# A list scheduler's latencies, landing time, buffer names and order table exchanged in a four-layer attention step

## The chip, the cores and the metric

The kernel runs on one core of a Trainium2 chip. The metric is device time in microseconds (us) of one execution; the median of three runs counts. The engines are named as the profile names them: PE is TensorE's matmuls, PEld its weight loads, DVE is VectorE, ACT is ScalarE, POOL is GpSimd, and SP issues every transfer of this kernel from one queue.

## The reference

One step of a model with four layers over 128 context tokens and 512 latent tokens of width 1024, all in float32. Layers 0 and 3 attend globally, layer 1 in a band with a sink logit, layer 2 in a two-dimensional neighbourhood with a bias table. Cut to what matters:

```python
for l in range(DEPTH):                      # the context tokens, then the latent ones
    shift, scl, gate = split(silu(cond) @ w_mod[l] + b_mod[l])
    u = rms_norm(h, norm_pre[l]) * (1 + scl) + shift
    q, k, v, z = split(u @ w_in[l])         # q: 16 heads of 64, k and v: 4 heads of 64
    q, k = rms_norm(q), rms_norm(k)         # per head; rotary positions for latent tokens
    o = softmax(q k^T / 8 [+ mask or bias]) v     # latent queries also read cached k and v
    h = h + gate * rms_norm((o * silu(z)) @ w_out[l], norm_post[l])
    # ... (k and v of the context tokens go out as a new cache)
```

## The kernel before

The 640 tokens are five tiles (tau) of 128; tile 0 is the context. The parts of a layer are functions named in `S.named`: `kv` projects k and v and stacks the transposed keys into `kst` (`k_stack`, its transposes are L553), `qt` projects and transposes q (products L497, transposes L620) for one half c of the heads, `z` makes the gate (L634), `pv` holds scores (L698, L724), softmax (maximum L701, exponential L703, scaling L658), the transposes of the probabilities p (L773) and the product with v (L780), `cx` does the context's heads (L800, L826, L834), `og` splits gated results, `no` and `out` multiply by w_out (L901), `un` and `up` normalize and shift the next layer's input (`mad` in `start_part`, L461 on ACT, L463 on DVE). `mod` and `mf` are the products with w_mod (L383; L346 for the first half of layer 0's), which need `cpad`, made from the tiny input `cnd` (L280, L282, L284, L285).

Float32 products are done as three products of a high and a low part. Each weight chunk of 128x512 comes into a `raw` tile, ACT rounds it (L261), DVE or POOL subtracts (L262). A PSUM result is copied out by ACT or DVE (`evac`, L256). There are four PSUM tiles `B`, two double ones `S`, and six `raw` tiles.

The program is not written in the order in which it runs. Every `S.op` lists the engines that could do a piece of work, with a price. `Sched.emit` then plays a list scheduler with these prices: it takes for each engine the ready operation with the least (start, key), where the key is the operation's number plus `ORDER[part]`, `MODSHIFT` or `SSHIFT`; it looks at most `WINDOW` operations ahead; a result counts as ready after the latency `LAT` of the pair of engines, a transfer so long after its end on the queue's model; `SLACK` favours keys over early starts, and `DISLIKE` handicaps a form of work on an engine that has an alternative (Ap and mada on ACT; V, V2 and mad on DVE; G and G1 on POOL). What it picks is emitted at once, so the playing decides each engine's order, SP's too, and which engine does what. At run time each engine keeps that order and waits by semaphores. Buffers of a kind come from a pool; the kernel's model only counted how many were free.

Of the kernel before, what the change touches and what calls it, by code (L numbers as in the profile page):

```python
# [25 lines left out]
           (([(0, (0, 2))], [(1, (0, 2))], [(0, (2, 4))], [(1, (2, 4))]),))  # L26


ORDER = {'hn': -470, 'up': -310, 'pv': 20, 'nat': 90, 'tab': -80, 'un': -170, 'bt': -280, 'st': -780, 'out': 230,
         'z': 90, 'og': -200, 'sc': 180, 'qt': -410, 'no': 180, 'ks': -170, 'mod': 160, 'w': -60}  # L30
MODSHIFT = 100
SSHIFT = -200
WINDOW = 520
PLAT = 270
XLAT = 180
SLACK = {'P': 140, 'V': 0, 'A': 220, 'G': 50, 'D': 80}
DISLIKE = {'Ap': 1060, 'mada': 3020, 'G1': 980, 'mad': 900, 'V': 1260, 'V2': 960, 'G': 780}
CAPS = {'p': 6, 'raw': 6, 'cap_prep': 3}
NEG = -1e30
KINDS = [0, 1, 2, 0]  # L40
# [7 lines left out]
class Buf:  # L48


    def __init__(self, tag, shape, dt):
        self.tag, self.shape, self.dt = tag, shape, dt
        self.ap = None
        self.ops = 0
        self.freed = 0.0
        self.hist = []


class Sched:

    LAT = {("P", "P"): 0, ("V", "V"): 130, ("A", "A"): 155, ("G", "G"): 110, ("P", "V"): 200, ("P", "A"): 200,
           ("G", "V"): 80, ("A", "V"): 110, ("V", "A"): 135, ("G", "A"): 150, ("D", "D"): 100, ("V", "P"): 235, ("A", "P"): 228}

# [58 lines left out]
    def emit(self):  # L126
# [5 lines left out]
            for d in deps:  # L132
                users[d].append(i)
        free = {e: 0.0 for e in "PVAGD"}
        slots = {t: [0.0] * c for t, (c, _) in self.tags.items()}
        done, where = [None] * n, [None] * n
        port = 0.0
        pend = {e: [] for e in "PVAGD"}
# [8 lines left out]
        out, low, last = 0, 0, "M"  # L147
        while out < n:
            while where[low]:
                low += 1  # L150
            best = None
            for e, lst in pend.items():
                cand = None
                for x in lst:
                    i = x[1]
                    if i > low + WINDOW or self.prev[i] is not None and where[self.prev[i]] is None:
                        continue
                    if x[3] is None:
                        t = 0.0
                        for d in self.ops[i][1]:  # L160
                            t = max(t, done[d] + (self.LAT.get((where[d], e), PLAT if e == "P" else XLAT)))
                        x[3] = t
                    t = max(x[3], free[e] + (self.TURN.get((last, x[2][3]), 0) if e == "P" else 0))
                    if e == "G" or x[2][3] in self.SHARED:
                        t = max(t, port)
                    need = {}
                    for b in self.ops[i][2]:
                        if b.ap is None:
                            m = need[b.tag] = need.get(b.tag, 0) + 1
                            s = slots[b.tag]  # L170
                            t = max(t, s[m - 1]) if len(s) >= m else 1e18
                    if t < 1e17:
                        key = (max(t, free[e] + SLACK[e]), x[0])
                        if cand is None or key < cand[0]:
                            late = DISLIKE.get(x[2][3], 0) if len(self.ops[i][0]) > 1 else 0
                            cand = (key, t, x, t + late)
                if cand and (best is None or cand[3] < best[0][3]):
                    best = (cand, e)
            if best is None:
                raise RuntimeError("no op can go")  # L180
            (_, t, x, _), e = best
            i, (_, dur, fn, _) = x[1], x[2]
            for alt in self.ops[i][0]:
                pend[alt[0]] = [y for y in pend[alt[0]] if y[1] != i]
            for b in self.ops[i][2]:
                if b.ap is None:
                    slots[b.tag].pop(0)
                    b.ap = self.tags[b.tag][1](b)
            fn(self.eng[e])
            free[e] = t + dur  # L190
            if e == "G" or x[2][3] in self.SHARED:
                port = t + dur
            if e == "P":
                last = x[2][3]
            done[i] = t + dur + (2000 if e == "D" else 0)
            where[i] = e
            for b in self.ops[i][2]:
                b.ops -= 1
                b.freed = max(b.freed, done[i])
                if not b.ops:  # L200
                    bisect.insort(slots[b.tag], b.freed + (215 if b.tag in ("S", "B") else 150))
            out += 1
            for u in users[i]:
                left[u] -= 1
                if not left[u]:
                    ready(u)


def build(ctx, tc, a, o):
# [5 lines left out]
    S = Sched(nc)  # L215

    def sbuf_tag(name, cap):
        S.tag(name, cap, lambda b: sb.tile(b.shape, b.dt, tag=name, name=name, bufs=cap))

    def psum_tag(name, cap):  # L220
        S.tag(name, cap, lambda b: pp.tile(b.shape, b.dt, tag=name, name=name, bufs=cap))

    for name, cap in (("gate", 1), ("q", 5), ("kst", 1), ("kn2", 1), ("vt", 1), ("w", 8),
                      ("raw", 4), ("p", 5), ("pt", 6), ("tmp", 6), ("tab", 1), ("gt", 1), ("modc", 4), ("bcol", 4),
# [738 lines left out]
    mod = mod_tile(0)  # L963
# [111 lines left out]
```

## Time and profile before

| what | value |
|---|---|
| runs | 1398.53, 1402.02, 1402.59 us; median 1402.02 |
| the profiled execution | 1400.58 us, of which 1398.5 us are the span from first to last instruction |
| PE busy | 1357.7 us, 97% of the span |
| PEld busy | 1122.3 us, 80% |
| DVE, ACT, POOL busy | 954.7, 758.6, 266.8 us (68, 54, 19%) |
| transfers | 145.11 MB, mean 104 GB/s |

A line of groups (such as "PE MATMUL B<-w,uB ... x816") has the engine, the operation, what it writes and reads, and how often. A timeline row has the start in us, the length in us, the engine, the kernel's line, and in brackets how long the engine sat idle before it and whose end released it. A matmul's end is modelled, so that a wait shorter than a matmul's pipeline does not show as idle time.

### The profile page before, as it was taken

The page shows a single profiled execution, that of the slowest core. Times are in us where ns is not written, and L with a number is a line of the kernel's source. Part 1 is how long each engine was busy: PE and PEld are TensorE (multiplying, and loading weights), DVE is VectorE, ACT ScalarE, POOL GpSimd, SP SyncE. Part 2 cuts the span into 40 slices and gives each one's busy share as a digit, 9 for nine tenths or more (in the row PEclk, how much of TensorE's full clock was granted, in tenths as well). Part 3 has the DMA queues.
Part 4 walks back from the last instruction along what each step waited for, and adds up shares of the span by engine and source line. Part 5 has one row for each costly group of instructions (what it writes and reads, how often), then busy time and mean ns, then how long its engine had stood idle before and what let it go on. Part 6 is the DMA issues. An engine that isn't in the chain of part 4 may idle for free.

```text
span 1398.5 us, 25496 instructions
## 1 busy us (share of the span) xinstructions
PE 1357.7 (97%) x9464; PEld 1122.3 (80%) x9464; DVE 954.7 (68%) x2300; ACT 758.6 (54%) x1854; POOL 266.8 (19%) x306
## 2 busy tenths in 40 slices
PE   6999999999999999999999999999999999999998
PEld 3788887888778887887878888888778888778876
DVE  4777667765587786777486676578488876577653
ACT  4556565554355565666354567468345555465641
POOL 1122012010032102201033541441033210021100
PEclk9999999999999999999999999999999999999999
DMA  8522222224532402324542522342633210111032
GB/s 305 175 69 84 61 91 84 69 87 140 181 115 67 147 30 91 125 92 161 161 125 73 157 57 91 98 141 85 196 126 101 91 53 10 61 52 41 31 123 103
DMA packets 73323, 145.11 MB, mean 104 GB/s; under 512 B 8752, under 2 KB 13936, under 8 KB 73200
## 3 DMA queue, kind: packets, MB, share of 16 engines
q1 hardware_dynamic: 73200, 143.50, 31.6%
q8 instruction: 74, 1.21, 0.4%
q14 instruction: 49, 0.40, 0.1%
HBM read 131.90 MB, written 11.57 MB: 103 GB/s over the span
## 4 chain that ended last, share of the span: by engine, by line
PE 83%; DVE 6%; ACT 4%; DMA 3%; issue 3%; POOL 0%; SPq 0%; DVEq 0%; POOLq 0%; ACTq 0%
PE B L497 21%; PE B L634 14%; PE B L780 8%; PE B L773 8%; PE S L901 8%; PE B L901 6%; PE S L698 5%; PE S L724 4%; PE B L383 3%; PE B L620 2%; PE S L497 1%; DVE w L262 1%; DMA raw<-in_w_mod 1%; DMA raw<-in_w_in 1%; PE B L451 1%
## 5 line engine op out<-in xcount | busy, mean ns | idle before, releaser
L307 POOL TENSOR_TENSOR sm<-sm,mhalf 128x1 f32<-128x1 f32 (+2 forms) x100 | 122.1, 1223 | 573.2 <-DVE sm L302 291.5
L497 PE MATMUL B<-w,uB 128*128 128x512 f32 x816 | 207.4, 401 | 0.0
L256 ACT ACTIVATE pt<-B 128x512 f32<-128x512 f32 (+1 forms) x228 | 126.9, 570 | 121.0 <-PE B L773 110.8
L497 PEld LDWEIGHTS B<-w,uB 128*128 128x128 f32 x816 | 149.2, 188 | 31.8 <-DVE uB L262 0.4
L634 PE MATMUL B<-uB,w 128*128 128x384 f32 x768 | 166.0, 348 | 0.6 <-DVE gate L642 0.3
L773 PE MATMUL B<-ident,p 128*128 128x128 f32 x1088 | 159.4, 276 | 3.1 <-ACT pt L256 2.3
L261 ACT ACTIVATE w<-raw 128x512 fp32r<-128x512 f32 x224 | 135.0, 627 | 30.2 <-PE B L901 8.0
L773 PEld LDWEIGHTS B<-ident,p 128*128 128x128 f32 x1088 | 125.1, 141 | 23.7 <-issue 13.6
L262 DVE TENSOR_TENSOR w<-raw,w 128x512 fp32r<-128x512 f32 x193 | 130.5, 700 | 13.0 <-ACT w L261 12.4
L497 PE MATMUL B<-w,uA 128*128 128x512 f32 x528 | 135.1, 403 | 1.1 <-DVE pt L256 0.8
L703 ACT ACTIVATE p<-S,sm 128x640 f32<-128x640 f32 x128 | 101.3, 794 | 59.6 <-DVE sm L701 54.6
L780 PE MATMUL B<-pt,vt 128*64 128x256 f32 (+1 forms) x1152 | 133.0, 376 | 0.0
L634 PEld LDWEIGHTS B<-uB,w 128*128 128x128 f32 x768 | 129.6, 188 | 3.7 <-issue 1.5
L701 DVE TENSOR_REDUCE sm<-S 128x1 f32<-128x640 f32 x128 | 102.7, 819 | 37.7 <-PE S L698 36.8
L634 PE MATMUL B<-uA,w 128*128 128x256 f32 x768 | 117.6, 290 | 0.3 <-DVE modc L394 0.3
L497 PEld LDWEIGHTS B<-w,uA 128*128 128x128 f32 x528 | 96.4, 188 | 24.7 <-DVE w L262 2.1
L780 PEld LDWEIGHTS B<-pt,vt 128*64 128x64 f32 x1152 | 77.5, 137 | 46.0 <-issue 11.4
L634 PEld LDWEIGHTS B<-uA,w 128*128 128x128 f32 x768 | 102.5, 189 | 3.4 <-issue 1.8
L658 DVE TENSOR_SCALAR p<-p,sm 128x640 f32<-128x640 f32 (+2 forms) x197 | 96.9, 506 | 6.6 <-DVE sm L657 0.5
L698 PE MATMUL S<-kst,q 128*128 128x320 f32 x512 | 96.8, 320 | 2.9 <-ACT p L703 2.8
L658 POOL TENSOR_SCALAR p<-p,sm 128x640 f32<-128x640 f32 (+2 forms) x59 | 44.0, 751 | 284.3 <-DVE sm L657 236.4
L737 ACT ACTIVATE p<-p,sm 128x512 f32<-128x512 f32 (+1 forms) x128 | 83.9, 657 | 6.4 <-DVE sm L735 6.3
(148 smaller groups left out, 2216.1 us busy)
## 6 DMA issues: line engine op xcount, KB each, us to landing
raw<-in_w_in SPq DMA_DIRECT2D x160, 256.0 KB
raw<-in_w_mod SPq DMA_DIRECT2D x160, 256.0 KB
raw<-in_w_out SPq DMA_DIRECT2D x64, 256.0 KB
w<-in_w_first SPq DMA_DIRECT2D x16, 512.0 KB
xs<-q SPq DMA_DIRECT2D x15, 512.0 KB
q<-xs SPq DMA_DIRECT2D x15, 512.0 KB
q<-in_x SPq DMA_DIRECT2D x10, 512.0 KB
kst<-gs SPq DMA_DIRECT2D x8, 512.0 KB
```

The source lines that it names most:

```text
L256: alts = {"A": Ap(n, lambda e: e.activation(out(), in_(), AF.Copy)), "V": V(n, lambda e: e.tensor_copy(out(), in_()))}
L261: S.op([As(n, lambda e: e.activation(h(), src(), AF.Copy))], r, w)
L262: f = lambda e: e.tensor_sub(l(), src(), h().bitcast(F32))
L307: S.op([("G", 395 + 157 * n, lambda e: e.tensor_tensor(r.ap, v.ap, mhalf.ap.to_broadcast([128, n]), op=OP.pow), "pow")], r=[v, mhalf], w=[r])
L497: e.matmul(ps(), t.ap[:, s, k, off:off + 128], W[k].ap[:, w], start=k == 0 and i == 0, stop=k == 7 and i == 2)
L634: e.matmul(ps.ap[:, 0:w], W[k].ap[:, wi, 128 * f:128 * f + 128], t.ap[:, s, k, :], start=k == 0 and i == 0, stop=k == 7 and i == 2)
L658: f = lambda e, i=i, p=p, w=w: e.tensor_scalar(p.ap[:, 0:w], p.ap[:, 0:w], rs.ap[:, i:i + 1], 1.0, op0=OP.mult, op1=OP.mult)
L698: e.matmul(ps.ap[:, b, 0:320], Q[t + 1].ap[:, hh], kst.ap[:, g, s, 320 * b:320 * b + 320], start=s == 0, stop=s == 1)
L701: S.op([V(640, lambda e, ps=ps, i=i: e.tensor_reduce(negm.ap[:, i:i + 1], ps.ap[:, :, 0:320], axis=AX.XY, op=OP.max, negate=True))], r=[ps ...
L773: e.transpose(pt.ap[:, c:c + 128], p.ap[:, b:b + 128], ident.ap)
L780: e.matmul(po.ap[64 * x:64 * x + 64, 256 * half + q0:256 * half + q0 + w], vt.ap[:, kt, 64 * g:64 * g + 64], sbt.ap[:, c0:c0 + w], start=f ...
L901: e.matmul(ps(), t.ap[:, s, k, off:off + 128], W[k].ap[:, w], start=k == 0 and i == 0, stop=k == 7 and i == 2)
```

## The change

Two constants' tables that the scheduler plays with (`LAT` and what stands in the first lines) get other numbers. A transfer counts as landed 4000 ns after its issue's end in the model, not 2000. A freed buffer now carries a slot number, and each slot has a name of its own in the memory pool, so that the buffer which the model hands out is the one that the program uses. No instruction's form is new, and no work is added or removed. The diff, with two lines of the order table:

```diff
-ORDER = {'hn': -470, 'up': -310, 'pv': 20, ... 'st': -780, 'out': 230,
+ORDER = {'mf': -5, 'tab': 1033, 'kv': -1015, ... 'hn': -2276, ... 'qt':
...
-MODSHIFT = 100
-SSHIFT = -200
-WINDOW = 520
+MODSHIFT = 38
+SSHIFT = -255
+WINDOW = 750
+LAND = 4000
-SLACK = {'P': 140, 'V': 0, 'A': 220, 'G': 50, 'D': 80}
-DISLIKE = {'Ap': 1060, 'mada': 3020, 'G1': 980, 'mad': 900, 'V': 1260, 'V2': 960, 'G': 780}
+SLACK = {'P': 98, 'V': 112, 'A': 190, 'G': 158, 'D': 16}
+DISLIKE = {'V2': 437, 'V': 4793, 'Ap': 663, 'G': 1355, 'mad': 1665, 'mada': 380, 'G1': 549}
...
-    LAT = {... ("P", "V"): 200, ("P", "A"): 200, ... ("V", "P"): 235, ("A", "P"): 228}
+    LAT = {... ("P", "V"): 210, ("P", "A"): 235, ... ("V", "P"): 150, ("A", "P"): 175, ...}
...
-        slots = {t: [0.0] * c for t, (c, _) in self.tags.items()}
+        slots = {t: [(0.0, k) for k in range(c)] for t, (c, _) in self.tags.items()}
...
-                    slots[b.tag].pop(0)
+                    b.slot = slots[b.tag].pop(0)[1]
...
-            done[i] = t + dur + (2000 if e == "D" else 0)
+            done[i] = t + dur + (LAND if e == "D" else 0)
...
-                    bisect.insort(slots[b.tag], b.freed + (215 if b.tag in ("S", "B") else 150))
+                    bisect.insort(slots[b.tag], (b.freed + (170 if b.tag in ("S", "B") else 190), b.slot))
...
-        S.tag(name, cap, lambda b: sb.tile(b.shape, b.dt, tag=name, name=name, bufs=cap))
+        S.tag(name, cap, lambda b: sb.tile(b.shape, b.dt, tag="%s%d" % (name, b.slot), name=name, bufs=1))
```

Nearly every row of the order moves. In the changed program each line number is four higher. These are the places that the prediction speaks of.

**The first transfers on SP.** Before:

```order
L280 DMA cnd<-in_cond 128x16
L329 DMA bcol<-in_vec 128x40
L296 DMA sink<-in_sink 128x16
L340 DMA w<-in_w_first 128x1024 x2
L969 DMA q<-in_x 128x1024
L340 DMA w<-in_w_first 128x1024 x2
```

And changed:

```order
L569 DMA tmp<-in_cache_k 128x128
L570 DMA kn_79<-in_cache_k 128x128
L571 DMA vt<-in_cache_v 128x256
L344 DMA w<-in_w_first 128x1024 x4
L284 DMA cnd<-in_cond 128x16
L333 DMA bcol<-in_vec 128x40
L300 DMA sink<-in_sink 128x16
L973 DMA q<-in_x 128x1024
```

The tiny `cnd`, first before, now stands behind three tiles of the cache and four of 512 KB.

**PE in layer 3, where the first half of the heads ends and the key stack of the second half is transposed** (L553 before, L557 now). Before:

```order
L800 MATMUL S<-kst,q 128x128 x8
L773 MATMUL B<-ident,p 128x128 x4
L634 MATMUL B<-uA,w 128x256 x9
L800 MATMUL S<-kst,q 128x128 x8
L773 MATMUL B<-ident,p 128x128 x8
L553 MATMUL B<-identr,tmp 128x128 x8
L780 MATMUL B<-pt,vt 64x256 x10
L553 MATMUL B<-identr,tmp 128x128 x16
L634 MATMUL B<-uB,w 128x384 x9
```

And changed:

```order
L804 MATMUL S<-kst,q 128x128 x8
L501 MATMUL B<-w,uA 128x512 x3
L784 MATMUL B<-pt,vt 64x256 x10
L557 MATMUL B<-identr,tmp 128x128 x4
L501 MATMUL B<-w,uA 128x512 x3
L557 MATMUL B<-identr,tmp 128x128 x8
L501 MATMUL B<-w,uA 128x512 x3
L557 MATMUL B<-identr,tmp 128x128 x8
L501 MATMUL B<-w,uA 128x512 x3
L557 MATMUL B<-identr,tmp 128x128 x4
```

The 24 transposes, in rows of 8 and 16, now come as 4, 8, 8 and 4 with three products of the next projection between them; the p transposes that stood straight ahead of them have gone further up.

**ACT at the same place.** Before:

```order
L640 ACTIVATE gate<-B 128x256
L809 ACTIVATE p,sm<-S,sm 128x128
L544 ACTIVATE tmp<-kn_11958 128x256 x6
L256 ACTIVATE pt<-B 128x512
L809 ACTIVATE p,sm<-S,sm 128x128
L256 ACTIVATE pt<-B 128x512
L256 ACTIVATE kst<-B 128x4x128
```

And changed:

```order
L644 ACTIVATE gate<-B 128x384
L265 ACTIVATE w<-raw 128x512
L260 ACTIVATE pt<-B 128x512
L813 ACTIVATE p,sm<-S,sm 128x128
L548 ACTIVATE tmp<-kn_11397 128x256 x6
L813 ACTIVATE p,sm<-S,sm 128x128 x3
L265 ACTIVATE w<-raw 128x512
L813 ACTIVATE p,sm<-S,sm 128x128
L260 ACTIVATE kst<-B 128x4x128
```

Two copies of transposed probabilities (`pt`) stood behind the six conversions of keys; now the last of them stands ahead.

**PE in layer 3, where the second half's scores begin.** Before:

```order
L698 MATMUL S<-kst,q 128x320 x4
L634 MATMUL B<-uA,w 128x256 x12
L773 MATMUL B<-ident,p 128x128 x4
L620 MATMUL B<-identr,tmp 128x128 x4
L634 MATMUL B<-uA,w 128x256 x6
L620 MATMUL B<-identr,tmp 128x128 x4
L698 MATMUL S<-kst,q 128x320 x4
L634 MATMUL B<-uB,w 128x384 x6
L383 MATMUL B<-raw,cpad 32x128 x16
```

And changed:

```order
L702 MATMUL S<-kst,q 128x320 x4
L638 MATMUL B<-uA,w 128x256 x9
L638 MATMUL B<-uB,w 128x384 x9
L638 MATMUL B<-uA,w 128x256 x3
L638 MATMUL B<-uB,w 128x384 x3
L638 MATMUL B<-uA,w 128x256 x6
L638 MATMUL B<-uB,w 128x384 x3
L638 MATMUL B<-uA,w 128x256 x6
L638 MATMUL B<-uB,w 128x384 x9
L624 MATMUL B<-identr,tmp 128x128 x8
L702 MATMUL S<-kst,q 128x320 x8
L777 MATMUL B<-ident,p 128x128 x4
L387 MATMUL B<-raw,cpad 32x128 x16
```

Between one score group and the next stood 18 gate products and two sets of transposes; now 48 gate products stand there, and the w_mod product (L383, now L387) comes later among them.

Which engine does a piece also changes. Of the 160 `mad` pieces of 128x128 all ran on DVE; 144 now run on ACT. ACT does 94 more copies out of PSUM, which is all that DVE did. DVE takes 24 subtractions (L262), 21 scalings (L658) and 8 small pieces from POOL. The matmuls are the same 8104 in both programs.

## Rows read from the trace of the kernel before

**Rows 1.** The page's span, its first part (busy us, share of the span, instructions) and the chain that ended last by engine.

```profile
span 1398.5 us, 25496 instructions
PE 1357.7 (97%) x9464; PEld 1122.3 (80%) x9464; DVE 954.7 (68%) x2300; ACT 758.6 (54%) x1854; POOL 266.8 (19%) x306
PE 83%; DVE 6%; ACT 4%; DMA 3%; issue 3%; POOL 0%; SPq 0%; DVEq 0%; POOLq 0%; ACTq 0%
```

**Rows 2.** Busy time of each engine in stretches that make up the span: the stretch, its length, then each engine's busy us, the granted clock, the transfers' share and GB/s.

```profile
0.00:50.00 50.00, 37.94 (x240) 24.15 (x240) 28.82 (x87) 21.20 (x53) 7.08 (x14) 1.00 0.85 302
50.00:200.00 150.00, 147.78 (x1131) 124.71 (x1130) 110.80 (x243) 88.99 (x208) 25.89 (x23) 1.00 0.24 77
200.00:250.00 50.00, 47.58 (x323) 39.46 (x322) 30.07 (x62) 24.47 (x51) 11.70 (x8) 1.00 0.26 84
250.00:1100.00 850.00, 841.50 (x5843) 697.65 (x5842) 595.78 (x1535) 473.48 (x1193) 188.27 (x227) 1.00 0.35 111
1100.00:1250.00 150.00, 141.51 (x1051) 118.42 (x1053) 102.44 (x207) 83.66 (x189) 23.09 (x19) 0.99 0.19 60
1250.00:1391.80 141.80, 141.40 (x890) 117.91 (x890) 84.58 (x166) 66.09 (x159) 10.18 (x14) 1.00 0.21 71
1391.80:1398.50 6.70, 0.01 (x1) 0.00 (x0) 2.23 (x4) 0.69 (x2) 0.55 (x1) 0.76 0.21 78
```

**Rows 3.** What PE waited for over the whole span: who waited, for whom, us in total, times, longest us.

```profile
PE B L346 <- DMA w<-in_w_first: 6.6, 2, 6.5
PE B L383 <- DMA raw<-in_w_mod: 3.4, 6, 1.2
PE S L698 <- ACT p L703: 2.8, 4, 1.0
PE B L773 <- ACT pt L256: 2.3, 5, 0.7
PE B L553 <- ACT pt L256: 1.9, 2, 1.6
```

**Rows 4.** The start: a stretch as in rows 2, then single rows of the timelines of ACT, DVE and PE.

```profile
6.00:12.00 6.00, 4.72 (x36) 1.76 (x36) 0.92 (x4) 1.60 (x5) 0.56 (x1) 1.00 1.03 387
2.35 0.22 ACT L282 ACTIVATE th<-cnd 128x16 f32<-128x16 f32 x1 [0.35 <-DMA cnd<-in_cond]
...
4.77 0.17 DVE L285 TENSOR_TENSOR cpad<-th,cnd 128x16 f32<-128x16 f32 x1
...
6.45 1.08 PE L346 MATMUL B<-w,cpad 128*32 128x256 f32 x8 [6.45 <-DMA w<-in_w_first]
7.71 1.08 PE L346 MATMUL B<-w,cpad 128*32 128x256 f32 x8 [0.17 <-DMA w<-in_w_first]
...
13.78 1.02 PE L353 MATMUL B<-sel,pm 128*128 128x2 f32 x4 [1.23 <-ACT pm L256]
...
17.01 1.65 PE L497 MATMUL S<-w,uA 128*128 128x512 f32 x3 [1.69 <-ACT uA L261]
...
22.41 0.66 PE L451 MATMUL B<-ident,q 128*128 128x128 f32 x2 [1.39 <-issue]
...
26.56 0.94 PE L497 MATMUL S<-w,uA 128*128 128x512 f32 x3
```

**Rows 5.** The end of the first half of the heads in layer 3: PE's timeline, then ACT's, then a stretch as in rows 2.

```profile
1191.76 0.53 PE L553 MATMUL B<-identr,tmp 128*128 128x128 f32 x4 [1.56 <-ACT pt L256]
...
1193.05 3.76 PE L780 MATMUL B<-pt,vt 128*64 128x256 f32 x20
...
1198.15 1.02 PE L553 MATMUL B<-identr,tmp 128*128 128x128 f32 x8 [0.36 <-ACT kst L256]
...
1205.54 3.08 PE L497 MATMUL B<-w,uA 128*128 128x512 f32 x12 [0.78 <-DVE pt L256]
...
1189.26 1.96 ACT L544 ACTIVATE tmp<-kn 128x256 fp32r<-128x256 f32 x6
1191.10 0.61 ACT L256 ACTIVATE pt<-B 128x512 f32<-128x512 f32 x1
...
1190.00:1200.00 10.00, 7.58 (x49) 4.93 (x48) 3.82 (x11) 7.09 (x22) 0.00 (x0) 0.83 0.00 0
```

**Rows 6.** PE's timeline where the second half's scores begin in layer 3, and one row of the first half's end with the same 20 products of p and v.

```profile
1242.73 0.54 PE L620 MATMUL B<-identr,tmp 128*128 128x128 f32 x4 [0.69 <-ACT pt L256]
...
1245.46 0.86 PE L698 MATMUL S<-kst,q 128*128 128x320 f32 x4 [0.96 <-ACT p L703]
...
1249.18 0.43 PE L383 MATMUL B<-raw,cpad 128*32 128x128 f32 x8 [1.24 <-DMA raw<-in_w_mod]
...
1182.38 2.38 PE L780 MATMUL B<-pt,vt 128*64 128x256 f32 x20
```

**Rows 7.** Groups of DVE, ACT and POOL by line and shape: busy us, mean ns of one, and the idle time before them.

```profile
L463 DVE TENSOR_SCALAR tmp<-B,modc 128x128 f32<-128x128 f32 x160 | 54.6, 401 | 8.1 <-PE B L451 7.9
L256 DVE COPY pt<-B 128x512 f32<-128x512 f32 x71 | 48.2, 685 | 12.9 <-PE B L773 11.4 <-PE B L826 0.7
L262 DVE TENSOR_TENSOR w<-raw,w 128x512 fp32r<-128x512 f32 x193 | 130.5, 700 | 13.0 <-ACT w L261 12.4
L256 ACT ACTIVATE pt<-B 128x512 f32<-128x512 f32 x169 | 100.2, 598 | 111.4 <-PE B L773 101.5 <-PE B L826 8.5
L256 ACT ACTIVATE pm<-B 128x128 f32<-128x128 f32 x11 | 3.0, 277 | 16.8 <-PE B L383 16.8
```

More of the change, by code (lines that the diff above doesn't have):

```diff
@@ L26 @@
            (([(0, (0, 2))], [(1, (0, 2))], [(0, (2, 4))], [(1, (2, 4))]),))
-ORDER = {'hn': -470, 'up': -310, 'pv': 20, 'nat': 90, 'tab': -80, 'un': -170, 'bt': -280, 'st': -780, 'out': 230,
-         'z': 90, 'og': -200, 'sc': 180, 'qt': -410, 'no': 180, 'ks': -170, 'mod': 160, 'w': -60}
-MODSHIFT = 100
-SSHIFT = -200
-WINDOW = 520
+ORDER = {'mf': -5, 'tab': 1033, 'kv': -1015, 'ks': -282, 'nat': 95, 'hn': -2276, 'mod': 295, 'w': 49, 'qt':
+         -2263, 'z': 101, 'sc': 286, 'st': -268, 'pv': -2148, 'cx': 109, 'og': 2620, 'out': -950, 'no': 290,
+         'un': -513, 'up': -1539, 'bt': -809, '': 32}
+MODSHIFT = 38
+SSHIFT = -255
+WINDOW = 750
 PLAT = 270
+LAND = 4000
 XLAT = 180
-SLACK = {'P': 140, 'V': 0, 'A': 220, 'G': 50, 'D': 80}
-DISLIKE = {'Ap': 1060, 'mada': 3020, 'G1': 980, 'mad': 900, 'V': 1260, 'V2': 960, 'G': 780}
+SLACK = {'P': 98, 'V': 112, 'A': 190, 'G': 158, 'D': 16}
+DISLIKE = {'V2': 437, 'V': 4793, 'Ap': 663, 'G': 1355, 'mad': 1665, 'mada': 380, 'G1': 549}
 CAPS = {'p': 6, 'raw': 6, 'cap_prep': 3}
@@ L53, in __init__ @@
         self.ap = None
+        self.slot = 0
         self.ops = 0
@@ L59 @@
 class Sched:
-    LAT = {("P", "P"): 0, ("V", "V"): 130, ("A", "A"): 155, ("G", "G"): 110, ("P", "V"): 200, ("P", "A"): 200,
-           ("G", "V"): 80, ("A", "V"): 110, ("V", "A"): 135, ("G", "A"): 150, ("D", "D"): 100, ("V", "P"): 235, ("A", "P"): 228}
+    LAT = {("P", "P"): 0, ("V", "V"): 120, ("A", "A"): 155, ("G", "G"): 110, ("P", "V"): 210, ("P", "A"): 235,
+           ("G", "V"): 35, ("A", "V"): 145, ("V", "A"): 130, ("G", "A"): 150, ("D", "D"): 100, ("V", "P"): 150, ("A", "P"): 175,
+           ("V", "G"): 150, ("A", "G"): 190}
     TURN = {("C", "M"): 179, ("E", "M"): 179, ("C", "T"): 132, ("E", "T"): 132, ("C", "R"): 132, ("E", "R"): 132, ("R", "M"): 45,
@@ L170, in emit @@
                             s = slots[b.tag]
-                            t = max(t, s[m - 1]) if len(s) >= m else 1e18
+                            t = max(t, s[m - 1][0]) if len(s) >= m else 1e18
                     if t < 1e17:
@@ L217, in sbuf_tag @@
     def sbuf_tag(name, cap):
-        S.tag(name, cap, lambda b: sb.tile(b.shape, b.dt, tag=name, name=name, bufs=cap))
+        S.tag(name, cap, lambda b: sb.tile(b.shape, b.dt, tag="%s%d" % (name, b.slot), name=name, bufs=1))
     def psum_tag(name, cap):
-        S.tag(name, cap, lambda b: pp.tile(b.shape, b.dt, tag=name, name=name, bufs=cap))
+        S.tag(name, cap, lambda b: pp.tile(b.shape, b.dt, tag="%s%d" % (name, b.slot), name=name, bufs=1))
     for name, cap in (("gate", 1), ("q", 5), ("kst", 1), ("kn2", 1), ("vt", 1), ("w", 8),
```

## The prediction

> **What bounds the kernel now.** I read the page's first part and its chain first: PE is busy for 1357.7 of 1398.5 us, and 83% of the chain that ended last is PE's own work [rows 1]. No other engine is over 68%. The matmuls are the same 8104 in both programs, so a new order cannot shorten this work; it can only take from the 40.8 us in which PE is idle (1398.5 less 1357.7), from waits too short to show as idle, and from the slow clock that follows idleness.
>
> The second view says where these 40.8 us are [rows 2]. Per stretch, length less PE's busy time: 12.1 us in the first 50 us; 2.2 from 50 to 200; 2.4 from 200 to 250; 8.5 in all of 250 to 1100; 8.5 in the 150 us from 1100 to 1250; 0.4 up to 1391.8; and 6.7 after the last matmul. The last 6.7 us are a chain of small steps and a transfer behind the last product, the last 72 products stand in the same order in both programs, and nothing changes there. So there are 22.0 us in the middle (2.2 + 2.4 + 8.5 + 8.5 + 0.4) and 12.1 at the start that an order can touch.
>
> The third view names what ended the idle times [rows 3]: at the start the transfers of w_first (6.6 us, of which 6.5 are the first wait); in the middle many short ones, the w_mod transfers (3.4 us), the exponentials of which a score tile must be free (2.8), copies of transposed probabilities out of PSUM (2.3 and 1.9). None is a rate that something lacks: the transfers run at 0.19 to 0.35 of their capacity in the middle [rows 2]. They are places where one queue held the wrong thing first, which an order can mend.
>
> **The change, part by part.**
>
> *The start.* `cpad`, which every `mod` product needs, hangs on `cnd`. Before, `cnd` is the first transfer and ACT takes it at 2.35 us; `cpad` is made at 4.77, and PE starts at 6.45, when the first w_first tile is there; the second is used at 7.71, 1.26 us later [rows 4]. Now `cnd` stands behind four such tiles and 0.26 MB of cache. Counted from the landing at 6.45 three more tiles take 3 x 1.26 = 3.8 us, the cache 0.26 MB / 387 GB/s = 0.7 us [rows 4], so `cnd` is there at about 10.9 us. A rounding (0.22), two DVE steps (0.17 each) and three hand-overs, some 0.9 us in all, follow: PE's first w_mod product starts at about 11.8 us, 5.3 us later than before. That is one end. What comes back: by 11.8 us two products' tiles are there together and x is close behind, so the waits that PE has after its start before (0.17, 1.23, 1.69 and 1.39 us, 4.5 in all [rows 4]) have no cause left except the one of 1.23, a copy on ACT. Their sum without it is 3.3 us. PE also works in one piece sooner: until 24.9 us three products take 1.65 us and from 26.56 on 0.94 [rows 4], which is the step from the 1.2 to the 2.4 GHz level; a denser run may bring it earlier or, starting later, not. I take +5.3 - 3.3 - 0.5 = +1.5 us, with ends of +5.3 (nothing comes back) and -2 (the clock rises some us earlier, too). A small PE transposition of cached keys now goes first and costs nothing, since PE idles there.
>
> The two w_first rows at 6.45 and 7.71 are in the order of issue, but show no small transfer behind a large one [rows 4]. The Trainium skill, "DMA: Bandwidth & Descriptors", section "Two DMAs through the same engine are not ordered", says that descriptors of one queue on one engine start in order, though they may finish otherwise. By that, the tiny transfer gets the full delay of the bytes ahead, as priced above, and the trace's two rows agree; if small transfers passed large ones, the start would stay as it was, and the sum below would be 1.5 us lower.
>
> *The end of a half in layer 3.* At 1189.26 ACT takes six key conversions in a row, 1.96 us; the copy `pt` that frees a PSUM tile waits behind them until 1191.10, and PE for the copy: 1.56 us of idle, then 0.36 and 0.78 [rows 5]. And the idleness costs twice: the mean granted clock falls to 0.83 of full over 1190 to 1200 [rows 5], and the 20 products at 1193.05 take 3.76 us where the same 20 took 2.38 just before [rows 5, 6], 1.4 us lost. In the changed order the `pt` copies stand ahead of the conversions on ACT, and PE has products of the next projection between its 4, 8, 8 and 4 transposes. I take all of it away: -(1.56 + 0.36 + 0.78 + 1.4) = -4.1 us. What is late next is the copies of `kst`, 0.6 us each, against 0.7 us of products in between: no wait over some tenths.
>
> *The scores of the second half.* At 1242.73, 1245.46 and 1249.18 PE waits 0.69, 0.96 and 1.24 us [rows 6]: a copy, an exponential, a w_mod tile. The same place in layer 0 gives most of the 2.4 us of 200 to 250 [rows 2]. Now 48 gate products stand between score groups where 18 stood, and the w_mod product comes later; the changed scheduler also holds a transfer as landed 2 us later. -(2.9 + 2.4) = -5.3 us.
>
> *The rest of the middle*, 22.0 - 2.7 - 2.9 - 2.4 = 14.0 us of idle in some forty short waits. The same rules were changed, but I have not followed each. I take half, -7.0 us, net of new waits; the ends are -14 (all gone) and +6 (none gone, and new ones as large as those of the two places above).
>
> *Work moved between engines.* DVE loses 144 `mad` pieces at 0.40 us and 94 copies, most of them at 0.69, and takes 24 subtractions at 0.70 and 21 scalings: about -58 - 58 + 17 + 12 = -87 us. ACT takes 144 pieces, whose nearest row is a 128x128 copy at 0.28, and 94 copies at up to 0.60: 40 + 52 = +92 us [rows 7]. ACT goes from 759 to 851 us, DVE from 955 to 868, both near 61 to 62% of the span. At a layer's start, where `mad` stands on the way to the first products, that is a relief for DVE; I cost it at nothing, because PE's own work covers both engines. If the cover goes, the price is the third rival's.
>
> *The names of buffers.* This makes the program's buffer the one that the model meant. It can save no more than waits for a reuse, the copies of rows 3, 4.2 us, of which I have already counted 1.56 and 0.69; taken at 0.
>
> Sum: +1.5 - 4.1 - 5.3 - 7.0 = -14.9 us. Against the profiled execution's own time of 1400.58 us that is 1385.7; that execution lies 1.4 us under the median of 1402.02, so about 1386 to 1387. I say 1386.
>
> **Rivals.**
>
> *More than half of the rest goes.* If all 14 us go and waits hidden in the matmuls' modelled ends shrink too: 1400.6 + 1.5 - 4.1 - 5.3 - 14 = 1379, and down to 1373 with the start's better end and a few us of hidden waits. For it: transfers and all engines have room [rows 2]. Against: the changed scheduler takes shorter latencies towards PE, so its order is tight, and a wait of 0.1 us times some hundred hand-overs gives back 10.
>
> *The start costs its full price.* +5.3 at the start and a quarter of the rest: 1400.6 + 5.3 - 4.1 - 5.3 - 3.5 = 1393. For it: the first 50 us move 302 GB/s at 0.85 of the transfers' time [rows 2], so lost time there is not simply made up.
>
> *Waits move and do not go.* PE's idle middle stays near 22 us, since a pipe that is emptied at one place is late at the next: 1400.6 +- 4. For it: the copies, exponentials and w_mod transfers in rows 3 all stand for a tile that is not yet free, and four PSUM tiles, two score tiles and six raw tiles are no more than before.
>
> *Slower: ACT becomes the one that PE waits for.* Place: softmax stretches, where ACT does exponentials, conversions of weights and now every copy out of PSUM. A copy that arrives while ACT is at a weight conversion waits on average half of about 0.6 us (a copy's own length [rows 7]); 94 moved copies x 0.3 = 28 us, if each reaches PE. It decides once more than half of them do (14 us, the whole gain); all of them give 1400 - 15 + 28 = 1413. Against: ACT is at 84 of 150 us in the stretch where PE waits most [rows 2], and its copies already wait for PE 101.5 us in total and not PE for them [rows 7].
>
> **How the numbers follow.** The forecast, 1380 to 1392, has 0.52. More than half goes (1370 to 1380): 0.16. The start's full price (1392 to 1397): 0.12. Waits move (1397 to 1406): 0.12. Slower by ACT: 0.08. About 0.3% of the median, 4.2 us, is what a measurement of this kernel can tell from no change, so faster means under 1397.8: 0.52 + 0.16 + 0.12 = 0.80; the same 0.12; slower 0.08. The range that leaves out 2 in 10 runs from 1374 (half of the first rival's lower part left out) to 1400.
>
> **What would show it.** PE's first w_mod product near 11.8 us, not 6.5; PE's busy time in the first 50 us within 2 us of 37.9; a granted clock of 1.0 at layer 3's change of halves; waits on w_mod tiles under 1 us in total; PE's idle middle at 10 to 12 us. I am wrong if the copies on ACT head the list of PE's waits, if PE's first 50 us lose 5 us more, or if idle time shrinks and the span does not, which would mean waits that the modelled ends hide.

## The result and the profile after

| | median us | runs | ratio to before, 95% interval |
|---|---|---|---|
| before | 1400.28 | 4 (1398.34 to 1402.59) | 1 |
| changed | 1368.42 | 4 (1367.44 to 1369.78) | 0.9773 [0.9751, 0.9794] |

The kernel is 32 us faster (the kernel before has one more run here than in its table above). 1386 was forecast, in a range from 1374 to 1400: the direction was right, the gain more than twice as large, and the time lies below the range.

First the changed kernel's span, its first part and the chain by engine, as in [rows 1].

```profile
span 1365.7 us, 25588 instructions
PE 1339.8 (98%) x9464; PEld 1116.9 (82%) x9464; DVE 879.3 (64%) x2115; ACT 839.2 (61%) x2092; POOL 211.4 (15%) x253
PE 94%; ACT 2%; DMA 1%; DVE 1%; issue 1%; SPq 0%; DVEq 0%; POOLq 0%; ACTq 0%
```

The span is 32.8 us shorter. PE's idle time went from 40.8 to 25.9 us (1365.7 less 1339.8), which is 14.9 us less. PE's busy time went from 1357.7 to 1339.8, 17.9 us less, with the same matmuls.

The stretches of [rows 2]: length, then busy us of PE, PEld, DVE, ACT and POOL, the granted clock, the transfers' share and GB/s.

```profile
0.00:50.00 50.00, 37.09 (x264) 24.68 (x265) 20.76 (x64) 32.78 (x88) 4.19 (x12) 1.00 0.84 307
50.00:200.00 150.00, 148.31 (x1113) 125.68 (x1111) 103.39 (x220) 95.76 (x228) 18.50 (x15) 1.00 0.24 76
200.00:250.00 50.00, 50.00 (x368) 42.40 (x369) 35.61 (x73) 27.48 (x60) 9.49 (x6) 1.00 0.31 100
250.00:1100.00 850.00, 845.78 (x5941) 706.56 (x5938) 555.84 (x1432) 531.68 (x1363) 154.95 (x199) 1.00 0.36 113
1100.00:1250.00 150.00, 150.00 (x1144) 127.81 (x1143) 101.26 (x208) 96.48 (x222) 16.18 (x11) 1.00 0.17 57
1250.00:1359.00 109.00, 108.66 (x645) 89.73 (x643) 60.22 (x117) 54.37 (x134) 7.51 (x10) 1.00 0.22 78
1359.00:1365.70 6.70, 0.00 (x0) 0.00 (x0) 2.23 (x4) 0.65 (x2) 0.55 (x1) 0.66 0.21 78
```

Idle per stretch is 12.9 at the start, 6.2 in the middle (1.7 + 0 + 4.2 + 0 + 0.3) and 6.7 at the end, against 12.1, 22.0 and 6.7. The 150 us from 1100, where PE idled 8.5 us before, have none.

What PE waited for, as in [rows 3]: us in total, times, longest.

```profile
PE B L350 <- DVE cpad L289: 7.9, 1, 7.9
PE B L557 <- ACT tmp L548: 3.2, 1, 3.2
PE S L501 <- ACT vt L585: 1.7, 2, 0.9
PE B L387 <- DMA raw<-in_w_mod: 1.6, 2, 1.4
PE B L357 <- ACT pm L260: 1.3, 3, 0.5
PE B L777 <- DVE gate L646: 0.7, 1, 0.7
```

The first two lines and the fifth are the start; the third falls at 53 and 58 us. The copies on ACT that headed the middle before are gone, as is the wait of score tiles for exponentials.

Layer by layer: single stretches from the start of one layer's last output product to that of the next, the first one from 62 us on; the same columns. Before:

```profile
62.00:398.96 336.96, 332.32 (x2428) 278.25 (x2427) 230.32 (x486) 183.87 (x427) 52.65 (x49) 1.00 0.30 98
398.96:722.59 323.63, 320.39 (x2271) 266.00 (x2269) 236.01 (x636) 185.35 (x489) 54.44 (x48) 1.00 0.34 109
722.59:1046.75 324.16, 319.52 (x2264) 266.22 (x2263) 218.00 (x589) 183.74 (x460) 99.31 (x147) 1.00 0.37 115
1046.75:1391.42 344.67, 335.67 (x2201) 279.36 (x2199) 229.96 (x474) 179.25 (x415) 51.73 (x46) 1.00 0.20 66
```

And changed:

```profile
62.00:383.19 321.19, 321.18 (x2385) 270.47 (x2384) 209.99 (x433) 195.37 (x463) 32.45 (x29) 1.00 0.30 98
383.19:703.46 320.27, 317.37 (x2264) 264.44 (x2263) 213.45 (x585) 203.50 (x543) 44.02 (x43) 1.00 0.35 110
703.46:1020.61 317.15, 315.84 (x2264) 265.10 (x2263) 202.99 (x560) 197.74 (x507) 84.64 (x130) 1.00 0.37 116
1020.61:1358.46 337.85, 337.65 (x2244) 284.35 (x2243) 221.73 (x454) 201.75 (x473) 42.49 (x35) 1.00 0.22 73
```

Layer 2, the third row, is the clean case: the same 2264 matmuls in both, 7.0 us less, of which only 3.3 are idle time. The other 3.7 us came out of PE's "busy" time. (Layers 0 and 3 do not hold the same work in both: 43 matmul records moved from one to the other.)

### The profile page after: what moved, and what is told of

It is laid out like the page before. It is cut to its first block, busy times and chain, and to the rows that moved or that the text cites. A ratio compares the mean times of both kernels' runs of the same rounds, so it can differ in the third digit from the quotient of the medians.

```text
span 1365.7 us, 25588 instructions
## 1 busy us (share of the span) xinstructions
PE 1339.8 (98%) x9464; PEld 1116.9 (82%) x9464; DVE 879.3 (64%) x2115; ACT 839.2 (61%) x2092; POOL 211.4 (15%) x253
## 4 chain that ended last, share of the span: by engine, by line
PE 94%; ACT 2%; DMA 1%; DVE 1%; issue 1%; SPq 0%; DVEq 0%; POOLq 0%; ACTq 0%
PE B L501 23%; PE B L638 16%; PE B L784 9%; PE B L777 9%; PE S L905 8%; PE B L905 7%; PE S L702 6%; PE S L728 4%; PE B L387 3%; PE B L624 2%; PE S L501 2%; PE B L455 1%; PE B L557 1%; DMA raw<-in_w_mod 1%; PE S L804 1%; PE B L350 1%
## 5 line engine op out<-in xcount | busy, mean ns | idle before, releaser
L260 ACT ACTIVATE pt<-B 128x512 f32<-128x512 f32 (+1 forms) x304 | 164.0, 576 | 97.3 <-PE B L777 88.9
L501 PE MATMUL B<-w,uB 128*128 128x512 f32 x816 | 202.7, 398 | 0.4 <-ACT q L260 0.4
L266 DVE TENSOR_TENSOR w<-raw,w 128x512 fp32r<-128x512 f32 x216 | 145.3, 691 | 21.2 <-ACT w L265 20.9
L777 PE MATMUL B<-ident,p 128*128 128x128 f32 x1088 | 152.5, 275 | 1.0 <-DVE gate L646 0.7
L638 PE MATMUL B<-uA,w 128*128 128x256 f32 x768 | 112.9, 285 | 0.0
L662 DVE TENSOR_SCALAR p<-p,sm 128x640 f32<-128x640 f32 (+2 forms) x218 | 106.6, 507 | 6.6
L662 POOL TENSOR_SCALAR p<-p,sm 128x640 f32<-128x640 f32 (+2 forms) x38 | 29.5, 778 | 350.9 <-DVE sm L661 209.2
```

The lines of the kernel that those rows point to most:

```text
L260: alts = {"A": Ap(n, lambda e: e.activation(out(), in_(), AF.Copy)), "V": V(n, lambda e: e.tensor_copy(out(), in_()))}
L266: f = lambda e: e.tensor_sub(l(), src(), h().bitcast(F32))
L501: e.matmul(ps(), t.ap[:, s, k, off:off + 128], W[k].ap[:, w], start=k == 0 and i == 0, stop=k == 7 and i == 2)
L638: e.matmul(ps.ap[:, 0:w], W[k].ap[:, wi, 128 * f:128 * f + 128], t.ap[:, s, k, :], start=k == 0 and i == 0, stop=k == 7 and i == 2)
L662: f = lambda e, i=i, p=p, w=w: e.tensor_scalar(p.ap[:, 0:w], p.ap[:, 0:w], rs.ap[:, i:i + 1], 1.0, op0=OP.mult, op1=OP.mult)
L777: e.transpose(pt.ap[:, c:c + 128], p.ap[:, b:b + 128], ident.ap)
```

## The experiments

Ratios are to the kernel before, measured beside each run; the changed kernel's is 0.9773. Differences between runs are taken from the ratios where they were not measured side by side.

**Which part brings the gain?** Eight runs take the change apart, one of them a control. The first has the slot numbers and a memory name per slot alone:

```diff
-        S.tag(name, cap, lambda b: sb.tile(..., tag=name, name=name, bufs=cap))
+        S.tag(name, cap, lambda b: sb.tile(..., tag="%s%d" % (name, b.slot), name=name, bufs=1))
...
```

> The kernel before with the slot numbers and a memory name per slot alone; every engine's order stays as it was. Theory A (the order took the waits away, names do next to nothing): 1400 us within 3, the three copies' waits of the reuse rows at most 1 us smaller. Theory B (the names, through the places of the buffers, also changed PE's pace from 234 to 232 ns per product of 512 columns): the pace is 232 ns in the last 72 products, and 1392 to 1394 us.

It took 1393.33 us, ratio 0.9954 [0.9938, 0.9970]: some 6 us less, with every engine's order as before. That is the time of Theory B, but not its pace: the last 72 products follow at 233.7 ns. The opposite, the changed kernel with that line back as it was:

> The changed kernel with the pool's old naming; every engine's order is the changed one. Theory A: 1368 us within 3. Theory B: the pace is back at 234 ns and the time at 1375 to 1377 us. If the pool takes another buffer than the model meant and that matters, PE's idle middle grows from 6 us by the waits for copies.

1370.77 us, 0.9798 [0.9779, 0.9818]. On the new order names are worth 2 to 4 us, within the intervals: the time of Theory A, though the pace moves most of the way to B's 234 (233.4 ns). Then the new numbers of the first lines alone, with the order, the shifts and the handicaps:

```diff
-WINDOW = 520
+WINDOW = 750
...
-SLACK = {'P': 140, 'V': 0, 'A': 220, 'G': 50, 'D': 80}
+SLACK = {'P': 98, 'V': 112, 'A': 190, 'G': 158, 'D': 16}
...
```

> The kernel before with the new order table, shifts, window, slacks and dislikes alone; old latencies, a transfer landed after 2000 ns, old names. If the tables carry the gain: 1368 to 1376 us, PE's idle middle 6 to 10 us. If table and latencies belong together: 1380 to 1395 us, with waits of PE for copies out of PSUM.

1407.53 us, 1.0057 [1.0039, 1.0076]: 0.6% slower. The kernel before once more, as the control:

> The kernel before, unchanged, on this chip, as a control of PE's pace. Theory B, and any in which the pace is the program's: 234 ns per product of 512 columns in the last 72, as in the first profile. If the pace belongs to the execution or the chip: another value, the same for all four kernels of this call.

1397.73 us; PE's busy time is 1356.1. The converse of the table's run, the changed kernel with the lines of that diff the other way round:

> The changed kernel with the old table of orders, shifts, window, slack and dislikes: new latencies, a landing of 4000 ns and the slot names stay. Theory 'the latencies carry it' (truer prices make any table play better): at most half of the 32 us is lost, 1370 to 1385 us. Theory 'table and latencies belong together' (the search fitted the table to these prices; the new table alone with the old prices cost 8 us): the gain is gone but for the names' 6 us or so, 1390 to 1405 us.

1393.79 us, 0.9939 [0.9919, 0.9959], no better than the names alone. So neither half carries the gain. Next, the changed kernel with the old latencies and times of release:

```diff
-    LAT = {... ("P", "A"): 235, ... ("V", "P"): 150, ("A", "P"): 175, ...}
+    LAT = {... ("P", "A"): 200, ... ("V", "P"): 235, ("A", "P"): 228}
...
-                    bisect.insort(slots[b.tag], (b.freed + (170 if b.tag in ("S", "B") else 190), b.slot))
+                    bisect.insort(slots[b.tag], (b.freed + (215 if b.tag in ("S", "B") else 150), b.slot))
```

> The changed kernel with the old latencies between engines and the old times after which a buffer is free; table, landing of 4000 ns and names stay. Theory 'the latencies carry it': within 3 us of the new table alone less the names, 1398 to 1406 us. Theory 'the later landing of transfers carries it': 1368 to 1380 us, since the landing stays. Theory 'table and latencies belong together': 1385 to 1405 us.

1377.81 us, 0.9830 [0.9807, 0.9854]. Of the three theories only the range of 'the later landing carries it' holds: most of the gain is still there, and 8 us are lost. Two runs take the landing up, with the new table and on the old one:

```diff
-            done[i] = t + dur + (2000 if e == "D" else 0)
+            done[i] = t + dur + (4000 if e == "D" else 0)
```

> The kernel before with the new table of orders, shifts, window, slack and dislikes and the landing of 4000 ns; old latencies, old names. With the landing left at 2000 ns the same table gave 1407.5 us. Theory 'table and later landing are a pair': 1379 to 1386 us, that is the 1377.8 us of the run with names plus what names are worth (2 to 6 us). Rival 'the table needs the fixed names': over 1395 us.

> The kernel before with one number changed, a transfer counts as landed after 4000 ns in place of 2000. Theory 'a later landing helps any table': 1378 to 1390 us. Theory 'it helps only the table found for it': 1397 to 1406 us, as the run with the old table and all the rest new (1393.8 us) is the names' 6 us or so better than before and no more.

With the new table 1378.12 us, 0.9847 [0.9816, 0.9877]; with the old one 1398.61, 0.9992 [0.9973, 1.0010]. So the landing does not carry the gain by itself either: the pair brings 21 us, the table alone loses 8, and the landing alone brings nothing that can be told from none. What PE waited for shows why; first the table alone, then table and landing:

```profile
PE B L347 <- DMA raw<-in_w_in: 7.8, 1, 7.8
PE B L498 <- DVE w L263: 3.9, 3, 1.3
PE B L384 <- DMA raw<-in_w_mod: 3.3, 4, 1.8
...
PE B L621 <- DVE gate L643: 2.6, 3, 0.9
```

```profile
PE B L347 <- DVE cpad L286: 7.7, 1, 7.7
PE B L554 <- ACT tmp L545: 3.1, 1, 3.1
PE B L384 <- DMA raw<-in_w_mod: 2.0, 2, 1.7
```

With 2000 ns the model puts products on PE whose weights (`w`, rounded from a transfer) are not there yet; with 4000 that wait for `w` and the one for `gate` are off the head of the list. The trace of the table alone also has three stretches of 3.4 us at half the clock (from 398, 698 and 729 us), the pair's has none.

**Is 4000 the point, and which latencies?** The changed kernel with one number each:

```diff
-LAND = 4000
+LAND = 3000
```

> The changed kernel with a landing of 3000 ns in place of 4000. Theory 'transfers land later than 2000 ns after their modelled end, the model has to allow for it, and by how much matters little': 1367 to 1373 us. Rival 'the gain of the later landing grows with its length': about half of the 29 us between the two runs of the new table alone, 1378 to 1388 us, with PE waiting on w_mod and w tiles again.

1375.43 us, 0.9820 [0.9803, 0.9837]: 7 us lost, between the two theories, and hardly by transfers: waits on w_mod are 2.4 us against 1.6. Its trace has more short waits for results of DVE and ACT, and one stretch of 3.4 us at half the clock (from 685 us), where the changed kernel's has none. The old latencies towards PE alone:

```diff
-    ("V", "P"): 150, ("A", "P"): 175,
+    ("V", "P"): 235, ("A", "P"): 228,
```

> The changed kernel with the old latencies towards PE alone (DVE to PE 235 for 150, ACT to PE 228 for 175). The prediction's argument against its own rival (the shorter ones make the order tight and give back up to 10 us): 1358 to 1366 us. Rival 'the shorter ones are nearer to the truth and let PE be filled closer': 1372 to 1378 us, most of the 9 us that all old latencies together cost. Third, no matter: 1367 to 1371 us.

1376.16 us, 0.9831 [0.9811, 0.9851]: nearly all of what the latencies are worth, and with the opposite sign to the prediction's argument.

**Is it one lucky order?** Two of the model's latencies nudged:

```diff
-    ("P", "V"): 210, ("P", "A"): 235,
+    ("P", "V"): 205, ("P", "A"): 225,
```

> The changed kernel with two latencies of the model made 5 and 10 ns shorter (PE to DVE 205, PE to ACT 225): no rule changes, about 5% of PE's rows stand elsewhere. Theory 'the rules carry it': within 3 us of the changed kernel, 1366 to 1372. Theory 'the search picked this one order': 1373 to 1385, as waits come back that the search had found a way around.

1370.10 us, 0.9771 [0.9746, 0.9795]: the same as the changed kernel. These two numbers need not be exact to 5 or 10 ns.

**Was the move from DVE to ACT free?** The changed kernel with the old handicaps:

```diff
-DISLIKE = {'V2': 437, 'V': 4793, 'Ap': 663, 'G': 1355, 'mad': 1665, 'mada': 380, 'G1': 549}
+DISLIKE = {'Ap': 1060, 'mada': 3020, 'G1': 980, 'mad': 900, 'V': 1260, 'V2': 960, 'G': 780}
```

> The changed kernel with the old handicaps alone, so that DVE gets its 160 pieces and most of its copies back. Theory of the prediction (the move between the engines is worth nothing, PE's work covers both): 1366 to 1373 us. Rival 'the move brings part of the gain, since DVE's conversions no longer queue behind copies': 1375 to 1385 us. Third, 'any number that leaves the set the table was found with costs as much as the old latencies did': 1376 to 1390 us.

1409.15 us, 1.0066 [1.0050, 1.0083]: 41 us lost, more than the whole gain and more than any theory said. DVE's busy time is back at 946.5 us. PE's waits:

```profile
PE B L624 <- DVE tmp L619: 3.1, 3, 1.5
...
PE B L501 <- DVE uB L266: 2.6, 3, 0.9
PE B L557 <- DVE sm L306: 2.3, 2, 1.1
```

Three of its largest are now for DVE, which the changed kernel's list does not have. But the old handicaps also give another order: from its 49th matmul on, PE's differs. So the 41 us are the price of the handicaps together with the order that they give, not of the busier DVE alone; in that order PE's work does not cover DVE. What the move would be worth with a table found for it was not tried.

**The start.** In the changed kernel alone, `cnd` issued first; then `cnd` and `sink`:

```diff
-    S.op([D(8, lambda e: e.dma_start(cnd.ap, a["cond"]))], w=[cnd])
...
+    nc.sync.dma_start(cnd.ap, a["cond"])
+    S.op([D(8, lambda e: None)], w=[cnd])
...
+    nc.sync.dma_start(sink.ap[:, 0], a["sink"].to_broadcast([128, 16]))
```

> The changed kernel with one transfer moved: the tiny cnd is issued first on the queue again, all other orders as they are. By the prediction's own start term PE's first w_mod product comes 3 to 5 us earlier, waits of 3 to 4 us return behind it, and the time falls by 1 to 2 us, to about 1367. Rival 'the start is bound by the stream of large transfers': the wait for cpad becomes a wait for the w_first tiles and the time stays within 0.7 us. Rival 'full price': 5 us less, 1363.

> The changed kernel with cnd and sink both issued ahead of all other transfers. (With cnd alone the wait for cpad stayed at 7.6 us, since DVE stood at the scaling of sink ahead of cpad until 11.65 us.) By the prediction's start term PE's first w_mod product comes 4 to 5 us earlier, about 3.3 us of waits return behind it, and the time falls by 1 to 2 us. Rival 'the stream of large transfers binds the start': the waits return in full and the time stays within 0.7 us of the changed kernel's. Rival 'full price': 4 to 5 us less.

1371.25 us, 0.9781 [0.9756, 0.9805], and 1367.02 us, 0.9765 [0.9738, 0.9792]: both the same as the changed kernel. In the first, DVE's queue kept `cpad` back behind `sink`. In the second PE's first w_mod product came at 7.49 us, and then PE waited:

```profile
7.49 2.27 PE L354 MATMUL B<-w,cpad 128*32 128x256 f32 x16 [2.03 <-DMA w<-in_w_first]
13.68 1.01 PE L361 MATMUL B<-sel,pm 128*128 128x2 f32 x4 [3.92 <-ACT pm L260]
14.62 1.93 PE L354 MATMUL B<-w,cpad 128*32 128x256 f32 x16
```

The second pair of tiles starts at 14.62, in the changed kernel at 15.42: of 4.55 us 0.8 is left. One trace cannot tell what becomes of that 0.8, because the clock rises to its higher level at another time in each. Nine products in this run and in the changed kernel:

```profile
24.05 4.19 PE L505 MATMUL S<-w,uA 128*128 128x512 f32 x9
```

```profile
24.05 2.33 PE L501 MATMUL S<-w,uA 128*128 128x512 f32 x9
```

The full clock is on record from 28.4 us here and from 23.2 in the changed kernel, but also from 26.5 and from 20.6 in two traces of the kernel before.

**PE's pace.** The last 72 products (512 columns) follow each other with nothing between them, in the same order everywhere. Their mean distance from start to start was 234.2 ns before, the same in the repeated run, and 232.0 changed (over the last 48 distances of the 71 alone it is 231.7, the figure of the expectations). A shift of all buffers by 64 bytes, the eight `w` tiles under one name again, and all buffers padded to multiples of 64 bytes (in the changed kernel and in the one before):

```diff
+    padt = sb.tile([128, 16], F32, tag="padt", name="padt", bufs=1)
...
+        if name == "w":
+            S.tag(name, cap, lambda b: sb.tile(b.shape, b.dt, tag=name, name=name, bufs=cap))
...
+            t = sb.tile([b.shape[0], -(-n // 16) * 16], ...)[:, 0:n]
```

> The changed kernel with an unused buffer of 64 bytes per partition in front of all others in SBUF, so that all of them lie 64 bytes further on; nothing else is changed. Theory 'PE's pace hangs on where the operands lie': the mean distance of the last 72 products leaves 231.7 ns by 0.5 ns or more and the time moves by 1 to 4 us. Rival 'the pace is set by the order and the naming, not by the place': 231.7 ns within 0.2 ns, time within 1.5 us.

> The changed kernel in which the eight w buffers alone share one memory name again, as before; order as changed. Theory 'where the w buffers lie sets PE's pace': the last 72 products go back to a distance that repeats every three products, mean 233.2 to 234.2 ns for 231.7, and the time rises by 1 to 4 us. Rival 'the pace has nothing to do with w': 231.7 ns within 0.3 ns, time within 1 us.

> The changed kernel with every buffer in SBUF padded to a multiple of 64 bytes per partition (before and after, w and the normalized inputs uA, uB start at odd multiples of 32 bytes in part); order, engines and names are the changed kernel's. Theory 'a product is faster where w and u both start at a multiple of 64 bytes' (in the run with one name for w both did for uB, and the last 72 products took 226.7 ns each; in the changed kernel only two of the eight w tiles did, and their products took 226 or 227): all 2400 products of 512 columns go from some 232.3 to 226.7 ns, 13 us less, 1353 to 1359 us. Rival 'only the sequence of w tiles counts': pace 231 to 234 ns, 1364 to 1370 us.

> The kernel before with every buffer in SBUF padded to a multiple of 64 bytes per partition; its order and names are kept. Theory 'a product is faster where w and u both start at a multiple of 64 bytes' (before, w does and u does not): the 2400 products of 512 columns go from 234.2 to 226.7 ns, 18 us less, 1380 to 1386 us, and the 6 us that names alone brought are then such a shift of places. Rival 'only the sequence of w tiles counts': 1397 to 1402 us.

| run | us | ratio | ns per product |
|---|---|---|---|
| shift by 64 bytes | 1367.63 | 0.9770 [0.9744, 0.9796] | 232.0 |
| one name for w | 1365.22 | 0.9748 [0.9734, 0.9763] | 227.2 |
| padded, changed | 1368.95 | 0.9768 [0.9747, 0.9790] | 232.0 |
| padded, before | 1393.93 | 0.9964 [0.9946, 0.9982] | 233.4 |

The last 72 products in PE's timeline before, changed, with one name for w, padded, and in the changed kernel with the old names for all:

```profile
1374.79 17.03 PE L901 MATMUL B<-w,uB 128*128 128x512 f32 x72
```

```profile
1341.99 16.87 PE L905 MATMUL B<-w,uB 128*128 128x512 f32 x72
```

```profile
1341.13 16.52 PE L908 MATMUL B<-w,uB 128*128 128x512 f32 x72
```

```profile
1343.65 16.87 PE L914 MATMUL B<-w,uB 128*128 128x512 f32 x72
```

```profile
1345.58 16.96 PE L905 MATMUL B<-w,uB 128*128 128x512 f32 x72
```

A shift of all buffers together changes nothing. With one name for `w` the order is the changed kernel's, and in the built program only `w` and some smaller buffers lie elsewhere (`uB` does not): each of these products takes 4.8 ns less in the mean, against the sign that was expected. It is the fastest kernel here, though its interval overlaps the changed kernel's. That the place counts, and not the sequence in which the eight `w` tiles are used, follows from the run with the old names. It has the same order, and by the built programs the same sequence of `w` tiles in these 72 products, but other places, and it takes 233.4 ns. The run with one name shows it within itself, too: after 62 us its products from `uB` into `B` follow each other at 228.2 ns, those from `uA` at 234.3; before, both take 234.

The rule of 64 bytes, drawn from that run, falls with the padded ones: padding leaves the changed kernel's pace where it was. The padded kernel before, with its own order and names, takes the 6 us that the names alone did, outside both ranges expected for it; its pace is 0.9 ns lower.

## Why the prediction was wrong

**The step that failed is the first paragraph's: of PE's idle time, "waits too short to show as idle" and the slow clock, only the shown idle time and 1.9 us of slow clock (1.4 in layer 3, 0.5 at the start) were priced.** What else PE's busy time could give was put at nothing, since a new order "cannot shorten this work"; 17.9 us came from it. The sum's −14.9 us equals what the shown idle time lost (40.8 to 25.9), but by luck in part: these 1.9 us are no idle time, and the 7.0 of the rest was a choice of half.

Where the busy time went is worked out from the trace: the distance from each matmul's start to the next one's, less the usual distance of that form and pair of lines in both kernels; over 60 ns is a wait. It is an estimate, since the usual distance can be the median or the lower quartile. Beyond 62 us the waits fall by 22 us by the one and 25 by the other, where the shown idle time there fell by 17.1 (the layers' rows): some 5 to 8 us of waits lay in the modelled ends, with the slow clock's among them. Differences under 60 ns fall by 9 or 7 us: the pace. The rest, the start included, makes about −2. Together that is −33.0, which is how much sooner the last matmul starts (1391.42 and 1358.46 us, the ends of the layers' rows).

How a wait hides shows in layer 2 before, in PE's timeline:

```profile
902.56 0.46 PE L620 MATMUL B<-identr,tmp 128*128 128x128 f32 x4
903.44 0.50 PE L620 MATMUL B<-identr,tmp 128*128 128x128 f32 x4 [0.41 <-DVE tmp L615]
```

and undisturbed in the changed kernel:

```profile
1192.12 0.45 PE L624 MATMUL B<-identr,tmp 128*128 128x128 f32 x4
1192.41 1.63 PE L501 MATMUL B<-w,uB 128*128 128x512 f32 x6
```

Four transposes let the next matmul start 0.29 us after their first; with the wait it is 0.88. That is 0.59 us lost, of which 0.41 is shown. Beyond 62 us there are 43 gaps over 0.1 us before. For 38 of them the same pair of lines also occurs without a wait; these hide 7.4 us, 0.16 to 0.27 each. In the changed kernel there are 9 such gaps, and 7 of them hide 1.4. The Trainium skill, "TensorE: Matmul & The Clock Gate", section "Step-by-step: what each phase is for", says that one matmul's drain is covered by the next one's fill only where they follow without a pause; the 0.16 to 0.27 us agree with that.

Point by point:

- **The start.** Forecast: `cnd` at about 10.9 us, the first w_mod product at about 11.8, +1.5 net. Measured: ACT takes `cnd` at 10.83, the product starts at 12.04, idle time is 0.8 us more, and PE is busy 37.09 us of the first 50 (37.9 before). Right, and the run with both tiny transfers first shows why it costs so little: the next waits take it up. (The 0.22 us called a rounding is the `tanh` of `cnd`; the sum is the same.) The term's 0.5 us for an earlier clock cannot be judged: the clock's rise moves by 6 us between two traces of the kernel before.
- **The end of a half in layer 3**, −4.1: right for the trace that it was read from. The last `pt` copy is ahead of the six conversions, and PE goes through; first ACT, then PE, then the stretch:

```profile
1172.32 0.60 ACT L260 ACTIVATE pt<-B 128x512 f32<-128x512 f32 x1 [0.33 <-PE B L777]
1173.16 1.94 ACT L548 ACTIVATE tmp<-kn 128x256 fp32r<-128x256 f32 x6
...
1173.74 2.38 PE L784 MATMUL B<-pt,vt 128*64 128x256 f32 x20
1176.05 0.54 PE L557 MATMUL B<-identr,tmp 128*128 128x128 f32 x4
1176.42 0.93 PE L501 MATMUL B<-w,uA 128*128 128x512 f32 x3
...
1160.00:1182.00 22.00, 22.00 (x166) 18.25 (x165) 15.63 (x32) 19.95 (x54) 0.00 (x0) 1.00 0.29 97
```

  The 20 products take 2.38 us, not the 3.76 of [rows 5], and the clock is 1.00. But the 1.4 us of slow clock belong to an execution and not to this place: in the second trace of the kernel before the clock stays at 1.00 here, and the 3.4 us at half the clock come with waits of 0.69 and 0.97 us in layer 0:

```profile
230.00:240.00 10.00, 8.31 (x67) 7.13 (x67) 9.02 (x20) 6.16 (x14) 4.96 (x3) 0.83 0.27 84
```

  Each trace of the kernel before has one such stretch, the changed kernel's has none before its last matmul.
- **The scores of the second half**, −5.3: right; 200 to 250 and 1100 to 1250 have no idle time.
- **The rest of the middle**, −7.0: of the 15.8 us, 2.7 + 2.9 + 2.4 belong to the two places, so 7.8 are the rest's. Right as shown idle time. That PE's idle middle would be 10 to 12 us did not follow from the sum, which left 7.0; it is 6.2. Waits on w_mod are 1.6 us, not under 1.
- **The move between engines**, at nothing: DVE and ACT came out at 879 and 839 us (868 and 851 said). But the term is not nothing here: with the old handicaps, and the order that they give, the kernel takes 41 us more.
- **Names**, at nothing: 2 to 4 us here, 6 on the old order. That they act there by where buffers lie, and not only by reuse, is likely and not shown: padding without names brought as much, and by the count above the differences under 60 ns fall by some 3.6 us in both traces.
- **The latencies.** The argument against the rival "more than half of the rest goes", that shorter latencies towards PE give back some 10 us, had the wrong sign: putting the old ones back costs 8. Of that rival the side clause came true, hidden waits, though its "few us" were too few; its main condition did not, since 7.8 of the 14 us of shown idle time went. The time lies below its 1373, too.

Not settled: why the landing's last 1000 ns are worth 7 us, though the waits on transfers hardly grew without them; what of a buffer's place sets the pace; and how the 7 to 9 us of pace divide between the names and the new order. In the changed order with the old names the same count gives 4 to 5 us.

## What to carry over

A PE that looks busy can hide the tail of each wait behind modelled ends: price each shown wait of PE with what its distance from start to start says, and look for waits that do not show at all. A scheduler's table, its prices and its choice of engines are one thing: measured part by part each may lose, so a part's worth alone says little of the whole. And a change of memory names moves buffers; pad or move them without the new names before crediting these.

## What was unexpected of the hardware

The same back-to-back products of 512 columns, in the same order, took 227.2, 232.0 or 233.4 ns in the mean, by where the buffers lie (one name for `w`, the changed kernel, the changed kernel with the old names), and two traces of the kernel before agree to 0.01 ns. Runs of 226 to 227 ns come where consecutive products have `w` and `uB` at the same remainder of 512 bytes in the built program: all eight `w` tiles with one name for `w`, and two neighbouring ones in the changed kernel and in its shifted copy. That was read afterwards from the last 72 products alone, and no run was made for it. It is not the whole of it: in the padded changed kernel 105 earlier products whose remainders differ by 64 took 228.4 ns in the mean, too.
